# Attention: the split of new queries and the SiLU of the gates issued half a slot later, behind the emptying of the transposed weights

## The chip, the cores and the metric

The kernel runs on one core of one Trainium2 chip. The metric is the device time of one execution in microseconds (us). A core has five engines with a queue each, and an engine takes its instructions in the order in which they were issued: TensorE (PE in the rows, its weight loads PEld), VectorE (DVE), ScalarE (ACT), GpSimd (POOL) and SyncE (SP), which issues the weights' transfers.

## The reference

A trunk of two layers over 256 tokens of width 2048: a gated linear recurrence (16 heads of 128) and a sparse attention with 16 query heads in 4 groups. The change lies in the attention, whose heads compute, for each of three branches (compressed keys, selected blocks, window):

```python
logit_c = jnp.einsum('bgqhd,bgkd->bgqhk', qb, K_cmp) + bias_shared(dist_c)
p_c = masked_softmax(logit_c, (dist_c >= 0)[:, None, :])
o_c = jnp.einsum('bgqhk,bgkd->bgqhd', p_c, V_cmp)
...
gates = jax.nn.sigmoid(gate_logits.reshape(B, S, NSA_HEADS, N_BRANCH))
o = jnp.einsum('bshc,bshcd->bshd', gates, out).reshape(B, S, NSA_WIDTH) * jax.nn.silu(z)
return o.astype(h.dtype) @ w_out
```

Queries `q` and gate inputs `z` come from columns of one input projection of the layer.

## The kernel before

All large products are done with each float32 operand split into a rounded part and a rest ("hi" and "lo", or names ending in `h` and `l`), and three products hi·hi, hi·lo, lo·hi (`mm3`, L154 to L156; in the transposed projections L179 and L181).

The program is one long list `plan` of weight pieces of 128x1024 elements. `flush` (L261) goes through it; a piece is a **slot**. In a slot it calls the `done` function of a finished projection, then `advance()`, then `prefetch` (which issues the hi cast of a piece three ahead on ScalarE, L138, the lo subtraction of a piece two ahead on VectorE, L148, and loads still further ahead), then the piece's matmuls on TensorE, then `advance()` again. Side work is written as Python generators, put in a list by `run`; `advance()` takes one step, up to the next `yield`, of each generator in the list, oldest first. One `yield` is thus half a slot, and the order of issue on each engine follows from where the `yield`s stand.

In the attention part the remaining projections (queries of groups 1 to 3, gates `z` of groups 0 to 3) run as pieces, and the heads run beside them as side work: `attend(g)` (L931) for a group of 4 heads. It keeps a table `turns` of half slots, a head taking 4 slots:

- `logits` of head h in the second half of slot 4h: 9 matmuls into three PSUM banks;
- `biased` (DVE) and `exps` (ACT) in slot 4h+1, `weigh` in slot 4h+2;
- `transposes` and `evacuate` in the second half of slot 4h+3. The seven transposed blocks stand in two banks: `t1` with four 128x128 blocks, `t2` with two, and with the 47x128 block of the compressed branch. `evacuate` (L996) empties them, ACT writing `ph` (hi) and `pc`, DVE `pl` (lo) and the other rows of `pc`;
- after each pair of heads (a = 0 or 1) `values` in the next two slots: half 0 needs the `ph` and `pl` of `t1` and the `pc` of the first token half (L1029), half 1 the rest.

`logits`, `transposes` and `values` share a ring of four PSUM banks (`psa`). So a matmul that opens a bank waits until the tile that had the bank four allocations earlier has been emptied. After head 1 the issue order is `logits` of head 2, then `values`: the third logits bank is that of `t1`, and the bank of `values` is that of `t2`. After head 3 `values` comes first, then the `logits` of the next group.

Two more generators run there. When half a query projection is finished, `q_done1` (L910) copies it out of PSUM, scales it and starts `q_split` (L920): ACT casts `qh` (L854), and two half slots later DVE subtracts `ql` (L862). When a gate projection is finished, `z_done1` (L1061) does the same with `z` and starts `gated` (L1070): ACT computes the SiLU of two 128x512 tiles (L1073) with a load of the SiLU table before it, and, for the first three groups, a one-element Exp (L1076) which brings the Exp table back; then the products with the heads' outputs (DVE, L1082) and their split into `yh` (ACT, L1085) and `yl` (DVE, L1087), which the output projection reads.

Of the kernel before, what the change touches and what calls it, by code (L numbers as in the profile page):

```python
# [8 lines left out]
F32 = mybir.dt.float32  # L9
# [25 lines left out]
NCMP = (S - CMP_BLOCK) // CMP_STRIDE + 1  # L35
# [10 lines left out]
def kernel(ctx: ExitStack, tc: tile.TileContext, x, norm_gains, final_gain, rel_bias,  # L46
                             hgrn_lb, hgrn_w_in, hgrn_head_gain, hgrn_w_out, nsa_w_in, nsa_pe_k, nsa_pe_v,
                             phi_k_w1, phi_k_b1, phi_k_w2, phi_v_w1, phi_v_b1, phi_v_w2, nsa_w_out, out):
    nc = tc.nc
# [801 lines left out]
    def split_of(src, hi, lo, col=None, apart=2):  # L851
        for s_, h in zip(src, hi):
            if col is None:
                nc.scalar.copy(h, s_)  # L854
            else:
                nc.scalar.activation(h, s_, AF.Copy, scale=col[0])
                col = col[1:] + col[:1]
        for _ in range(apart):
            yield
        for s_, h, l in zip(src, hi, lo):  # L860
            if col is None:
                nc.vector.tensor_sub(l, s_, h.bitcast(F32))  # L862
            else:
                nc.vector.scalar_tensor_tensor(l, s_, col[0], h.bitcast(F32), op0=ALU.mult, op1=ALU.subtract)
                col = col[1:] + col[:1]
# [44 lines left out]
    def q_done1(g):  # L910
        def done(a, ps):
            q = zs_take(ps)
            nc.vector.tensor_mul(q, q, rbq2)
            run(q_split(g, a, q))
            if g == 0 and a == 1:
                for n in range(G):
                    run(attend(n), HEAD * G * n + 13)
        return done

    def q_split(g, a, q):  # L920
        NS["q", g, a] = [NS["p2"].tile([P, 2, S], F32R, tag="q" + part, name="q" + part, bufs=3) for part in "hl"]
        yield from split_of([q], *([t] for t in NS["q", g, a]))

# [7 lines left out]
    def attend(g):  # L931
# [64 lines left out]
        def evacuate(h):  # L996
            t1, t2 = L.pop(("t", h))
            a, hh = h // 2, h % 2
            ph, pl = pT[a]
            srcs = ((t1.rearrange("p (a t) -> p a t", a=4), slice(0, 4)),  # L1000
                    (t2[:, 0:256].rearrange("p (a t) -> p a t", a=2), slice(4, 6)))
            pc = NS["pc"][:, hh]
            for t, ks in srcs:
                nc.scalar.copy(ph[:, ks, hh, :], t)  # L1004
            for tt in range(2):
                nc.scalar.copy(pc[64:64 + NCMP, tt], t2[32 * tt:32 * tt + NCMP, 256:384])  # L1006
            for t, ks in srcs:
                nc.vector.tensor_sub(pl[:, ks, hh, :], t, ph[:, ks, hh, :].bitcast(F32))  # L1008
            nc.vector.tensor_copy(pc[0:NCMP], pc[64:64 + NCMP].bitcast(F32))
            for tt in range(2):  # L1010
                nc.vector.tensor_sub(pc[32:32 + NCMP, tt], t2[32 * tt:32 * tt + NCMP, 256:384],  # L1011
                                     pc[64:64 + NCMP, tt].bitcast(F32))

        def values(a, half):
            if half == 0:
# [25 lines left out]
        for h in range(4):  # L1041
            at(HEAD * h, 1, logits, h)
            at(HEAD * h + 1, 0, biased, h)
            at(HEAD * h + 1, 1, exps, h)
            at(HEAD * h + 2, 0, weigh, h)
            at(HEAD * h + 3, 1, transposes, h)
            at(HEAD * h + 3, 1, evacuate, h)
        for a in range(2):
            n = HEAD * (2 * a + 2)
# [11 lines left out]
    def z_done1(g):  # L1061
        def done(a, ps):
            z = zs_take(ps)
            nc.vector.tensor_mul(z, z, rb2)
            NS["z", a] = z
            if a == 1:
                run(gated(g, [NS["z", 0], z]))
        return done

    def gated(g, zs):  # L1070
        ks = [slice(4 * g + 2 * a, 4 * g + 2 * a + 2) for a in range(2)]
        for a in range(2):
            nc.scalar.activation(zs[a], zs[a], AF.Silu)  # L1073
        if g + 1 < G:

            nc.scalar.activation(NS["one"], NS["one"], AF.Exp, scale=0.0)  # L1076
        yield
        yield
        for a in range(2):
            while ("out", g, a) not in NS:  # L1080
                yield
            nc.vector.tensor_mul(zs[a], zs[a], NS["o", g][:, a])  # L1082
            yield
            yield
            nc.scalar.copy(yh[:, ks[a]], zs[a])  # L1085
            yield
            nc.vector.tensor_sub(yl[:, ks[a]], zs[a], yh[:, ks[a]].bitcast(F32))  # L1087
# [147 lines left out]
```

## Time and profile before

| | us |
|---|---|
| median of 3 runs | 986.13 |
| lowest, highest | 985.73, 987.29 |
| the profiled execution's own time | 986.4 |
| its span, first to last instruction | 984.6 |
| TensorE busy in the span | 968.7 |
| VectorE, ScalarE, GpSimd busy | 658.3, 569.5, 59.9 |
| attention heads (690 to 897 us): TensorE busy of 207 us | 200.54 |

The profiled execution took 1.8 us more than its span, and lies 0.27 us above the median of the runs. Matmuls are pipelined: a matmul's row begins before the one ahead of it has ended, so a stretch in which TensorE is always "busy" may still hide some of a wait. The rows of the weight loads (PEld) show a wait more plainly: normally one starts every 0.12 us.

### The profile page before, as it was taken

The numbers are of one execution on the slowest core, as the hardware profiler recorded it, in microseconds if no ns is written. First come the engines' busy times: TensorE is split into PE (matmuls) and PEld (weight loads), VectorE is DVE, ScalarE is ACT, GpSimd is POOL, SyncE is SP. The second block draws the span as 40 slices with busy tenths as digits, with TensorE's granted clock in tenths as the row PEclk, the third lists the DMA queues.
The fourth block names the chain that finished last, engine by engine and source line by source line (L and its number), as shares of the span: only waits on it lengthen the run. The fifth ranks groups of instructions, "written<-read, shape, count | busy, mean of one in ns | idle before, by whom it ended". The sixth has DMA issues, their size and how long they took to land.

```text
span 984.6 us, 17622 instructions
## 1 busy us (share of the span) xinstructions
PE 968.7 (98%) x6735; PEld 838.5 (85%) x6735; DVE 658.3 (67%) x1275; ACT 569.5 (58%) x1056; POOL 59.9 (6%) x154
## 2 busy tenths in 40 slices
PE   9999999999999999999999999999999999999996
PEld 8888888888888888888888888998888888888886
DVE  6796478646864786465566666567777778686654
ACT  6754565456545654554455555467677776875542
POOL 3101000100010001000020000000000000000000
PEclk9999999999999999999999999999999999999999
DMA  9655565556555655566777776565555545546662
GB/s 317 201 172 151 172 192 165 157 171 193 156 166 172 186 158 163 176 222 231 234 218 207 223 229 184 157 198 170 150 152 141 158 130 160 160 130 232 204 215 96
DMA packets 141524, 178.98 MB, mean 182 GB/s; under 512 B 6016, under 2 KB 102880, under 8 KB 141312
## 3 DMA queue, kind: packets, MB, share of 16 engines
q1 hardware_dynamic: 139424, 171.86, 56.8%
q0 software_dynamic: 1680, 5.46, 2.0%
q8 instruction: 53, 0.87, 0.4%
q10 hardware_dynamic: 336, 0.54, 0.1%
q14 instruction: 31, 0.25, 0.1%
HBM read 173.62 MB, written 4.22 MB: 181 GB/s over the span
## 4 chain that ended last, share of the span: by engine, by line
PE 80%; ACT 10%; DVE 6%; issue 2%; DMA 1%; SPq 0%; POOLq 0%; ACTq 0%; POOL 0%; DVEq 0%
PE mainps L156 40%; PE mainps L179 21%; PE mainps L181 11%; PE auxps L156 3%; ACT L L970 2%; ACT hi L138 2%; PE auxps L516 2%; DVE lo L148 1%; DVE L L963 1%; ACT ph L1004 1%; ACT L L979 1%; ACT pc L1006 1%; DMA xt<-in_x_dram 1%; DVE pc L1011 1%; ACT L1073 1%
## 5 line engine op out<-in xcount | busy, mean ns | idle before, releaser
L179 PE MATMUL mainps<-xx,hi 128*128 128x512 f32 x1280 | 454.9, 398 | 0.2 <-DVE Kg L313 0.2
L138 ACT CAST hi<-raw 128x1024 fp32r<-128x1024 f32 (+3 forms) x317 | 328.0, 1039 | 206.6 <-PE mainps L156 142.8
L148 DVE TENSOR_TENSOR lo<-raw,hi 128x1024 fp32r<-128x1024 f32 (+3 forms) x317 | 379.2, 1206 | 92.1 <-ACT hi L138 91.3
L181 PE MATMUL mainps<-xx,lo 128*128 128x256 f32 x1280 | 357.6, 279 | 0.1
L179 PEld LDWEIGHTS mainps<-xx,hi 128*128 128x128 f32 x1280 | 240.2, 188 | 54.6 <-DVE Kg L313 0.6
L181 PEld LDWEIGHTS mainps<-xx,lo 128*128 128x128 f32 x1280 | 241.4, 189 | 0.6 <-DVE lo L148 0.4
L156 PE MATMUL mainps<-hi,xx 128*128 128x512 f32 (+1 forms) x704 | 209.4, 375 | 0.0
L156 PEld LDWEIGHTS mainps<-hi,xx 128*128 128x128 f32 x704 | 128.4, 188 | 23.2
L156 PE MATMUL mainps<-lo,xx 128*128 128x512 f32 (+1 forms) x352 | 131.0, 372 | 0.0
L156 PE MATMUL mainps<-hi,yh 128*128 128x512 f32 (+1 forms) x288 | 106.0, 368 | 0.0
L156 PE MATMUL mainps<-hi,yl 128*128 128x512 f32 (+1 forms) x288 | 105.4, 366 | 0.0
L156 PE MATMUL mainps<-lo,yh 128*128 128x512 f32 (+1 forms) x288 | 105.3, 366 | 0.0
L156 PEld LDWEIGHTS mainps<-lo,xx 128*128 128x128 f32 x352 | 66.1, 188 | 10.4
L156 PEld LDWEIGHTS mainps<-hi,yl 128*128 128x128 f32 x288 | 54.3, 189 | 8.8
L156 PEld LDWEIGHTS mainps<-lo,yh 128*128 128x128 f32 x288 | 54.4, 189 | 8.5
L156 PEld LDWEIGHTS mainps<-hi,yh 128*128 128x128 f32 x288 | 54.4, 189 | 8.4
L970 ACT ACTIVATE L<-L,mx 128x128 f32<-128x128 f32 (+1 forms) x96 | 37.6, 393 | 31.0 <-DVE mx L965 31.0
L313 DVE TENSOR_TENSOR zs<-mainps,zs 128x256 f32<-128x256 f32 x48 | 19.0, 421 | 33.7 <-ACT zs L311 33.7
L567 POOL COPY ST<-S 32x128 f32<-32x128 f32 x32 | 21.6, 675 | 229.8 <-DVE S L524 228.8
L524 DVE COPY_PREDICATED S<-masks,auxps 128x128 f32<-128x128 uint32 x48 | 14.6, 303 | 28.8 <-PE auxps L557 15.9
L1008 DVE TENSOR_TENSOR pl<-auxps,ph 128x512 fp32r<-128x512 f32 (+1 forms) x32 | 17.7, 557 | 22.0 <-ACT ph L1004 20.4
L311 ACT COPY zs<-mainps 128x256 f32<-128x256 f32 x48 | 16.5, 373 | 13.5 <-PE mainps L181 13.2
(257 smaller groups left out, 905.2 us busy)
## 6 DMA issues: line engine op xcount, KB each, us to landing
raw<-in_hgrn_w_in_dram SPq DMA_DIRECT2D x127, 512.0 KB, 4.0
raw<-in_nsa_w_in_dram SPq DMA_DIRECT2D x104, 512.0 KB, 3.8
raw<-in_hgrn_w_out_dram SPq DMA_DIRECT2D x32, 512.0 KB, 4.7
raw<-in_nsa_w_out_dram SPq DMA_DIRECT2D x32, 512.0 KB, 4.0
raw<-in_nsa_w_in_dram SPq DMA_DIRECT2D x10, 420.0 KB, 3.9
xt<-in_x_dram SPq DMA_DIRECT2D x8, 256.0 KB, 7.9
raw<-in_x_dram SPq DMA_DIRECT2D x4, 512.0 KB, 4.2
x_dram<-x POOLq DMA_DIRECT2D x4, 512.0 KB, 6.0
```

Of the source, the lines that this page charges most:

```text
L138: nc.scalar.copy(hi[:, :m], raw[:, :m])
L148: nc.vector.tensor_sub(lo[:, :m], raw[:, :m], hi[:, :m].bitcast(F32))
L156: nc.tensor.matmul(dst, a, b, start=first and n == 0, stop=last and n == 2, skip_group_check=True)
L179: nc.tensor.matmul(ps, hv[:, fs], xx[:, k].rearrange("p a t -> p (a t)"), start=k == 0, stop=False, skip_group_check=True)
L181: nc.tensor.matmul(ps[:, S:], lv[:, fs], xh[:, k], start=False, stop=k == KT - 1, skip_group_check=True)
L311: nc.scalar.copy(o, p[:, S:])
L313: nc.vector.tensor_add(o, p[:, :S], o)
L516: nc.tensor.matmul(dst[32 * b:32 * b + 32, j] if cols == 32 else dst[32 * b:32 * b + 32, :, j], k[:, cs], qs, start=True, stop=True, tile_ ...
L524: nc.vector.copy_predicated(S32, masks[:, i, None, :].to_broadcast([P, 4, 32]), bank[:, n])
L567: nc.gpsimd.tensor_copy(ST[rs, :, 0:3:2, rs], S32[rs].rearrange("p (h t) c -> p h t c", h=2))
L970: nc.scalar.activation(dst, dst, AF.Exp, bias=mx[:, i:i + 1], accum_out=sm[:, i:i + 1])
L1008: nc.vector.tensor_sub(pl[:, ks, hh, :], t, ph[:, ks, hh, :].bitcast(F32))
```

## The change

Three edits, all in the order of issue. No instruction is added or taken away, and no DMA changes.

```diff
     def q_split(g, a, q):
+        yield
         NS["q", g, a] = [...]
         yield from split_of([q], *([t] for t in NS["q", g, a]))
...
-            for t, ks in srcs:
+            for n, (t, ks) in enumerate(srcs):
                 nc.scalar.copy(ph[:, ks, hh, :], t)
-            for tt in range(2):
-                nc.scalar.copy(pc[64:64 + NCMP, tt], t2[32 * tt:32 * tt + NCMP, 256:384])
-            for t, ks in srcs:
+                for tt in range(2 - 2 * n):
+                    nc.scalar.copy(pc[64:64 + NCMP, tt], t2[32 * tt:32 * tt + NCMP, 256:384])
+            for n, (t, ks) in enumerate(srcs):
                 nc.vector.tensor_sub(pl[:, ks, hh, :], t, ph[:, ks, hh, :].bitcast(F32))
-            nc.vector.tensor_copy(pc[0:NCMP], pc[64:64 + NCMP].bitcast(F32))
-            for tt in range(2):
-                nc.vector.tensor_sub(pc[32:32 + NCMP, tt], ...)
+                if n == 0:
+                    nc.vector.tensor_copy(pc[0:NCMP], pc[64:64 + NCMP].bitcast(F32))
+                for tt in range(2 - 2 * n):
+                    nc.vector.tensor_sub(pc[32:32 + NCMP, tt], ...)
...
     def gated(g, zs):
         ks = [...]
+        yield
         for a in range(2):
             nc.scalar.activation(zs[a], zs[a], AF.Silu)
```

So the `qh` cast and the SiLU block are issued in the second half of a slot instead of the first, after `evacuate` of that half slot; everything that follows them in their generators (`ql`; the products with the heads' outputs, `yh`, `yl`) moves by the same half slot. Inside `evacuate`, on both engines, the `pc` parts now stand between the part of `t1` and that of `t2`.

The lines above L921 keep their numbers; below, the changed kernel's are 2 to 5 higher (L1004 becomes L1007, L1006 L1009, L1008 L1011, L1009 L1013, L1011 L1015, L1073 L1078, L1076 L1081, L1082 L1087).

**ScalarE, from the end of a gate projection to the first half of the next head's softmax** (after head 1 of groups 1 to 3; `zs` is the projection's tile, `auxps` a bank of the ring, `one` the one-element Exp). Before:

```order
L311 COPY zs<-mainps 128x256 x2
L1073 ACT_TABLE_LOAD
L1073 ACTIVATE zs<-zs 128x512 x2
L1076 ACT_TABLE_LOAD
L1076 ACTIVATE one<-one 128x1
L138 CAST hi<-raw 128x1024
L1004 CAST ph<-auxps 128x4x128
L1004 CAST ph<-auxps 128x2x128
L1006 CAST pc<-auxps 15x128 x2
L138 CAST hi<-raw 128x1024
```

Now:

```order
L311 COPY zs<-mainps 128x256 x2
L138 CAST hi<-raw 128x1024
L1007 CAST ph<-auxps 128x4x128
L1009 CAST pc<-auxps 15x128 x2
L1007 CAST ph<-auxps 128x2x128
L1078 ACT_TABLE_LOAD
L1078 ACTIVATE zs<-zs 128x512 x2
L1081 ACT_TABLE_LOAD
L1081 ACTIVATE one<-one 128x1
L138 CAST hi<-raw 128x1024 x2
```

Four instructions and the table loads have moved from ahead of the emptying to behind it, and now stand ahead of two weight casts and of the next exponentials.

**VectorE, at the same place.** Before:

```order
L148 TENSOR_TENSOR lo<-raw,hi 128x1024
L1008 TENSOR_TENSOR pl<-auxps,ph 128x4x128
L1008 TENSOR_TENSOR pl<-auxps,ph 128x2x128
L1009 CAST pc<-pc 15x256
L1011 TENSOR_TENSOR pc<-auxps,pc 15x128 x2
L1082 TENSOR_TENSOR zs<-zs,ot 128x512
L148 TENSOR_TENSOR lo<-raw,hi 128x1024
```

Now:

```order
L148 TENSOR_TENSOR lo<-raw,hi 128x1024
L1011 TENSOR_TENSOR pl<-auxps,ph 128x4x128
L1013 CAST pc<-pc 15x256
L1015 TENSOR_TENSOR pc<-auxps,pc 15x128 x2
L1011 TENSOR_TENSOR pl<-auxps,ph 128x2x128
L148 TENSOR_TENSOR lo<-raw,hi 128x1024
L1087 TENSOR_TENSOR zs<-zs,ot 128x512
```

The two-block part of `pl` is now last, and the product with the heads' output stands behind the next weight's lo part.

**ScalarE, from the end of half a query projection** (after head 3 of groups 0 to 2). Before:

```order
L311 COPY zs<-mainps 128x256 x2
L854 CAST qh<-zs 128x512
L138 CAST hi<-raw 128x1024
L1004 CAST ph<-auxps 128x4x128
L1004 CAST ph<-auxps 128x2x128
L1006 CAST pc<-auxps 15x128 x2
```

Now:

```order
L311 COPY zs<-mainps 128x256 x2
L138 CAST hi<-raw 128x1024
L1007 CAST ph<-auxps 128x4x128
L1009 CAST pc<-auxps 15x128 x2
L1007 CAST ph<-auxps 128x2x128
L854 CAST qh<-zs 128x512
```

The `qh` cast has moved behind the emptying; the weight's hi cast stays ahead of it. On TensorE, GpSimd and SyncE all instructions keep their order.

## Rows read from the trace of the kernel before

**Rows 1.** The profile page: its first line, and section 1 (busy time of each engine, its share of the span, its instructions).

```profile
span 984.6 us, 17622 instructions
...
PE 968.7 (98%) x6735; PEld 838.5 (85%) x6735; DVE 658.3 (67%) x1275; ACT 569.5 (58%) x1056; POOL 59.9 (6%) x154
```

**Rows 2.** Busy time of each engine by stage of the span (the view of windows): the attention heads, and the tail after the last projection. Columns: stretch in us from the span's start, its length, then busy us and instructions of PE, PEld, DVE, ACT, POOL, then granted clock, DMA share, GB/s.

```profile
690.00:897.00 207.00, 200.54 (x1230) 177.34 (x1229) 157.98 (x434) 149.46 (x359) 6.33 (x20) 1.00 0.52 152
...
975.00:984.60 9.60, 2.23 (x19) 2.02 (x17) 3.34 (x9) 1.05 (x2) 0.55 (x1) 0.85 0.57 218
```

**Rows 3.** The waits of TensorE's weight loads (PEld) over the whole span, the four that lie in the attention heads: engine, line and tile, what they waited for, us in total, times, longest us.

```profile
PEld auxps L156 <- DVE pl L1008: 3.4, 6, 0.7
PEld auxps L156 <- ACT hi L138: 3.2, 3, 1.1
PEld auxps L1029 <- ACT hi L138: 2.1, 4, 0.6
...
PEld auxps L156 <- ACT ph L1004: 0.9, 2, 0.5
```

**Rows 4.** The same view for TensorE's matmuls (PE), the three longest in the attention heads.

```profile
PE auxps L156 <- DVE pc L1011: 2.7, 3, 0.9
PE auxps L156 <- DVE pl L1008: 2.0, 6, 0.5
PE auxps L1029 <- ACT hi L138: 1.4, 4, 0.4
```

**Rows 5.** Timeline of TensorE's matmuls at the first of the places called one, in the second head group: the first and the last of the seven transposes of head 1. Columns of this and the next groups: start us, us, engine, line, operation, out<-in, shapes, xcount, and in brackets the idle time of the engine before it and what ended it.

```profile
735.81 0.60 PE L990 MATMUL auxps<-ident,L 128*128 128x128 f32 x4
...
736.46 0.27 PE L993 MATMUL auxps<-ident,L 128*47 128x128 f32 x1
```

**Rows 6.** Timeline of TensorE's weight loads at the same place: the last two that run undisturbed, the two that waited, and the first of the next head's transposes.

```profile
739.77 0.19 PEld L156 LDWEIGHTS auxps<-Kl,qh 128*128 128x128 f32 x1
739.90 0.19 PEld L156 LDWEIGHTS auxps<-Kh,ql 128*128 128x128 f32 x1
740.66 0.19 PEld L156 LDWEIGHTS auxps<-Kh,qh 128*128 128x128 f32 x1 [0.57 <-DVE pl L1008]
...
742.16 0.19 PEld L156 LDWEIGHTS auxps<-ph,Vsh 128*128 128x128 f32 x1 [1.08 <-ACT hi L138]
...
752.87 0.48 PEld L990 LDWEIGHTS auxps<-ident,L 128*128 128x128 f32 x4
```

**Rows 7.** Timeline of ScalarE (ACT) at the same place.

```profile
733.85 0.65 ACT L311 COPY zs<-mainps 128x256 f32<-128x256 f32 x2
734.51 1.28 ACT L1073 ACT_TABLE_LOAD   x1
735.81 1.15 ACT L1073 ACTIVATE zs<-zs 128x512 f32<-128x512 f32 x2
...
738.37 1.03 ACT L138 CAST hi<-raw 128x1024 fp32r<-128x1024 f32 x1
739.31 0.85 ACT L1004 CAST ph<-auxps 128x512 fp32r<-128x512 f32 x2
740.17 0.53 ACT L1006 CAST pc<-auxps 15x128 fp32r<-15x128 f32 x2
...
745.64 0.40 ACT L970 ACTIVATE L<-L,mx 128x128 f32<-128x128 f32 x1 [1.27 <-DVE mx L965]
...
748.61 0.91 ACT L979 ACTIVATE L<-L,sm 128x256 f32<-128x256 f32 x2 [0.52 <-DVE sm L976]
```

**Rows 8.** Timeline of VectorE (DVE) at the same place.

```profile
735.65 1.22 DVE L148 TENSOR_TENSOR lo<-raw,hi 128x1024 fp32r<-128x1024 f32 x1
739.92 1.24 DVE L1008 TENSOR_TENSOR pl<-auxps,ph 128x512 fp32r<-128x512 f32 x2 [3.05 <-ACT ph L1004]
741.17 0.28 DVE L1009 CAST pc<-pc 15x256 fp32r<-15x256 f32 x1
741.47 0.58 DVE L1011 TENSOR_TENSOR pc<-auxps,pc 15x128 fp32r<-15x128 f32 x2
742.08 0.69 DVE L1082 TENSOR_TENSOR zs<-zs,ot 128x512 f32<-128x512 f32 x1
```

**Rows 9.** Timeline of the weight loads at the first of the places called two that has three waits, after head 3 of the same group.

```profile
770.07 0.19 PEld L156 LDWEIGHTS auxps<-ph,Vsh 128*128 128x128 f32 x1 [0.48 <-ACT ph L1004]
770.80 0.19 PEld L156 LDWEIGHTS auxps<-pl,Vsh 128*128 128x128 f32 x1 [0.54 <-DVE pl L1008]
...
772.00 0.19 PEld L1029 LDWEIGHTS auxps<-pc,Vc 79*128 79x128 f32 x1 [0.55 <-ACT hi L138]
```

**Rows 10.** Timeline of ScalarE at that place.

```profile
766.05 0.65 ACT L311 COPY zs<-mainps 128x256 f32<-128x256 f32 x2
767.97 0.62 ACT L854 CAST qh<-zs 128x512 fp32r<-128x512 f32 x1 [1.27 <-DVE zs L913]
...
769.45 0.84 ACT L1004 CAST ph<-auxps 128x512 fp32r<-128x512 f32 x2
```

**Rows 11.** Timeline of VectorE at that place.

```profile
767.85 1.22 DVE L148 TENSOR_TENSOR lo<-raw,hi 128x1024 fp32r<-128x1024 f32 x1
770.05 1.24 DVE L1008 TENSOR_TENSOR pl<-auxps,ph 128x512 fp32r<-128x512 f32 x2 [0.98 <-ACT ph L1004]
...
771.60 0.59 DVE L1011 TENSOR_TENSOR pc<-auxps,pc 15x128 fp32r<-15x128 f32 x2
```

More of the change, by code (lines that the diff above doesn't have):

```diff
@@ L1002, in evacuate @@
             pc = NS["pc"][:, hh]
-            for t, ks in srcs:
+            for n, (t, ks) in enumerate(srcs):
                 nc.scalar.copy(ph[:, ks, hh, :], t)
-            for tt in range(2):
-                nc.scalar.copy(pc[64:64 + NCMP, tt], t2[32 * tt:32 * tt + NCMP, 256:384])
-            for t, ks in srcs:
+                for tt in range(2 - 2 * n):
+                    nc.scalar.copy(pc[64:64 + NCMP, tt], t2[32 * tt:32 * tt + NCMP, 256:384])
+            for n, (t, ks) in enumerate(srcs):
                 nc.vector.tensor_sub(pl[:, ks, hh, :], t, ph[:, ks, hh, :].bitcast(F32))
-            nc.vector.tensor_copy(pc[0:NCMP], pc[64:64 + NCMP].bitcast(F32))
-            for tt in range(2):
-                nc.vector.tensor_sub(pc[32:32 + NCMP, tt], t2[32 * tt:32 * tt + NCMP, 256:384],
-                                     pc[64:64 + NCMP, tt].bitcast(F32))
+                if n == 0:
+                    nc.vector.tensor_copy(pc[0:NCMP], pc[64:64 + NCMP].bitcast(F32))
+                for tt in range(2 - 2 * n):
+                    nc.vector.tensor_sub(pc[32:32 + NCMP, tt], t2[32 * tt:32 * tt + NCMP, 256:384],
+                                         pc[64:64 + NCMP, tt].bitcast(F32))
         def values(a, half):
```

## The prediction

> **What bounds the kernel now.** I read the page first, then the busy time by stage, then who waited for whom, then the timelines at the waits. The page shows TensorE busy 968.7 of 984.6 us [rows 1]: it is the bound, and a change that neither adds nor removes work can only give back the time in which TensorE stands still. By stage, 7.4 us of that are the tail (9.60 less 2.23), which the change does not reach, and 6.5 us (207.00 less 200.54) lie in the attention heads [rows 2], where all moved instructions are. The granted clock is 1.00 there, its upper level (2.4 GHz), so no time is lost to the clock.
>
> The view of waits then names the reasons: in that stage TensorE waits for the emptying of the transposed weights, and hardly for anything else. The matmuls' rows add to 2.7 + 2.0 + 1.4 = 6.1 us [rows 4]. The weight loads' rows add to 3.4 + 3.2 + 2.1 + 0.9 = 9.6 us in 15 waits [rows 3]. I take the second: at the first wait the loads before it start 0.13 us apart (739.77, 739.90), the next at 740.66 [rows 6], so about 0.64 us were really lost, where the load's row says 0.57. A load lasts 0.19 us and normally overlaps the next one by 0.07, so each wait costs 0.07 us more than its row: 9.6 + 15 x 0.07 = **10.6 us**, all that can be won here. The Trainium skill ("Perfetto Trace Analysis", Identifying the Most-Contended Engine) has the rule for this: matmul busy time is a poor measure since matmuls are pipelined, the weight loads are the better row. By the matmuls' rows the same argument would give 986.1 - 6.1, or 980.0 us; this trace sides with the rule, by the 0.64 us against 0.57 just read.
>
> **Places one: three times, after head 1 of groups 1 to 3.** ScalarE ends the copies of the gate projection at 734.50. Then the SiLU block (table load, two SiLUs, table load, Exp) runs to 738.37, 3.9 us, then a weight cast of 1.03, and only then, at 739.31, the emptying [rows 7]. But the transposes had ended at 736.41 (first four) and 736.73 (all) [rows 5]. VectorE stood idle 3.05 us before its part [rows 8]. TensorE lost 0.57 us at the third logits bank, which was still `t1`'s, and 1.08 us at the bank of `values`, still `t2`'s [rows 6].
>
> The new order, from the same durations. ScalarE: copies to 734.50, weight cast to 735.55, then it waits for the transposes; `ph`, `pc`, `ph` from 736.45 take 0.85 + 0.53, to 737.85 (was 740.70). VectorE: its lo part ends at 736.87 [rows 8]; the first `pl` starts when the first `ph` is written. As the two casts take 0.85 us for 512 and 256 columns, I put the first at 0.6, to 737.05. From there 1.24 + 0.28 + 0.58, with seams 2.2 us, to 739.2; the `t1` part is done by 737.9. TensorE wants the third logits bank at 739.90 + 0.12 = 740.02 and, three matmuls later, the bank of `values` at 740.4. Both are free by then, with 2.1 and 1.2 us to spare. So a place one gives all of 0.57 + 1.08 + 2 x 0.07 = 1.8 us, three times 5.4.
>
> What then stands in front of other work? The SiLU block ends at 737.85 + 3.9 = 741.75, two weight casts (1.03 each) at 743.8, and the next head's exponentials can start there. They started at 745.64 before [rows 7]; as TensorE is now 1.8 us further on, that is the same place against TensorE. The later scaling had ended at 748.61 + 0.91 = 749.52, and the transposes that need it were loaded at 752.87 [rows 6, 7]: 3.3 us of room, less 0.6 for the `yh` cast that now also goes ahead of the scaling (taken as the 0.62 of `qh`, of the same shape [rows 10]). `gated`'s product on VectorE comes up at 739.2 + 1.2 (a lo part) = 740.4, when its SiLU (737.85 + 1.28 + 0.6) has just ended at 739.8, so it does not hold up the queue. The two delayed weight casts make pieces three slots ahead; they end about 1 us later than before and have over two slots of room. I cost these at nothing.
>
> The Trainium skill ("ScalarE: Activation LUTs", What ACT_TABLE_LOAD costs) speaks against this part: a switch of table costs about 1283 ns plus a drain of about 1380 ns. The row has 1.28 us and the SiLU starting 1.30 us after the load began, no drain [rows 7]. With the page's drains, an estimate, the block would be 2.8 us longer; behind the emptying it would use up the 2.7 us of room just counted. The sum would stay, the rival on the slow side would be likelier. I go by the row.
>
> **Places two: after head 3 of each group.** Before, at the second of the four: copies to 766.70, `qh` waits for VectorE and starts at 767.97, weight cast, `ph` at 769.45 [rows 10]; TensorE waits 0.48 for `ph`, 0.54 for `pl`, 0.55 for `pc` [rows 9]. New: weight cast to 767.75, first `ph` 768.3, `pc` 768.85, second `ph` 769.2. VectorE is free at 767.85 + 1.22 = 769.07 [rows 11]; by columns the first `pl` takes two thirds of 1.24, to 769.9 at the latest, the copy of `pc` 0.28, to 770.2 [rows 8], the first `pc` part 0.3, to 770.5. TensorE would come at 770.07 - 0.48 = 769.6 for `ph`, 0.12 later for `pl`, and after six loads, at 770.3, for `pc`. So `ph` is in time, and about 0.2 us remain where VectorE is now the later one. Of the four places, the first has the `pc` wait alone (its VectorE is earlier), two have all three, and the last has two; it has a SiLU block in front instead of `qh`. Together they hold 10.6 - 5.4 = 5.2 us. I leave 0.5 of it standing: 0.2 at each of the two, 0.1 at the others. The reordering inside the emptying is in this: `pc` no longer waits for the second `pl` (a third of 1.24, 0.4 us). Alone it would save that at `pc` waits only; a bank waits for the last part whatever the order.
>
> `qh` behind the emptying is needed late: these queries serve heads 2 and 3 of the next group, eight slots on. The other half's split, moved after head 2, is needed one head later. SyncE's, GpSimd's and TensorE's orders are unchanged and no DMA moves; DMA is busy 0.52 in this stage [rows 2].
>
> **Sum.** 10.6 - 0.5 = 10.1 us. Against the profiled execution, 986.4 - 10.1 = 976.3; the median of the runs is 0.27 lower, so **976.0 us**. A measurement of this kernel can tell about 0.2%, 2 us, from no change.
>
> **Rivals.** (a) *Partly*: at places two VectorE turns into the bound. For: its lo part, 1.22 us, ends 1 us before TensorE arrives. Against: 0.2 us left by the working above. If half of their 5.2 us and a little at places one stays, 7.5 us are won: 978.6. (b) *No change*: the weight cast that still stands ahead of the emptying is itself held, and the SiLU hid it. It ran at 738.37 without a recorded wait [rows 7]; were it held until then, the emptying would start as late as before. The code says that it needs a buffer freed by the piece ahead of the one whose matmuls precede the transposes at 735.81 [rows 5], so it is ready well before them. The time would be 986.1. (c) *Slower*: what was moved now delays the softmax, and the transposes come late. If there were no room, three SiLU blocks of 3.9 us and six `qh` of 0.62 would all be paid: 15.4 us against 10.1, at 991.4. It decides where the exponentials start over 2.7 us later than reckoned. Against: rows 6 and 7 show the room. That the change does not do what it says is excluded by the order of issue, which shows both moves.
>
> **How the numbers follow.** The forecast, 975.0 to 977.5, gets 0.77; (a) 0.13; (b) 0.05; (c) 0.05. The low end is all 10.6 us and 0.5 for the spread of the runs; to hold 8 in 10 the range reaches into (a), to 979.5. Faster by over 0.2%: 0.77 + 0.13 = 0.90; within: 0.05; slower: 0.05.
>
> **What would show it.** In the profile after, the four weight-load waits of rows 3 shrink from 9.6 to under 1 us; `ph` starts within 0.1 us of the first four transposes at places one; the idle 3.05 us of VectorE before `pl` is gone; TensorE is busy over 99% of the heads' stretch, which is 10 us shorter. I am wrong if waits of the same size appear at `logits` or `values` behind other names, if a weight load waits for a hi or lo part, or if the transposes wait for ScalarE's scaling.

## The result, and the profile after

| us | before | after |
|---|---|---|
| median | 986.11 | 976.56 |
| lowest, highest | 985.73, 987.29 | 975.33, 977.63 |
| the profiled execution's own time | 986.4 | 976.73 |
| its span | 984.6 | 974.9 |

The median of before is that of four runs, one more than the table ahead of the prediction had. The changed kernel is faster: the ratio of after to before is 0.9901, with a 95% interval of 0.9884 to 0.9918. The forecast was 976.0, its range 975.0 to 979.5.

The profile page after: the span, the busy times, and (section 4) the shares of the engines in the chain that ended last.

```profile
span 974.9 us, 17621 instructions
...
PE 964.1 (99%) x6735; PEld 837.4 (86%) x6735; DVE 655.8 (67%) x1275; ACT 569.0 (58%) x1056; POOL 60.0 (6%) x154
...
PE 96%; DMA 1%; DVE 1%; issue 1%; ACT 0%; SPq 0%; POOLq 0%; POOL 0%; DVEq 0%
```

The same line of the page of before:

```profile
PE 80%; ACT 10%; DVE 6%; issue 2%; DMA 1%; SPq 0%; POOLq 0%; ACTq 0%; POOL 0%; DVEq 0%
```

So ScalarE and VectorE have all but gone from the chain. By stage (view of windows, columns as in rows 2): the heads, the tail.

```profile
690.00:887.30 197.30, 197.30 (x1232) 177.09 (x1232) 156.01 (x434) 148.84 (x359) 6.35 (x20) 1.00 0.54 162
...
965.30:974.90 9.60, 1.80 (x16) 1.59 (x14) 2.91 (x8) 0.72 (x1) 0.55 (x1) 0.74 0.57 219
```

The heads' stretch is 197.3 us where it was 207.0 [rows 2], at the same granted clock of 1.00, and TensorE stands still in none of it. The tail is as long as before. The waits of the weight loads over the whole span, the first and the third longest entries (columns as in rows 3):

```profile
PEld auxps L516 <- issue: 6.0, 17, 0.8
...
PEld auxps L1198 <- DVE zeros L321: 1.1, 1, 1.1
```

None of the four entries of [rows 3] is left; what stands here lies outside the heads. Place one in the second head group, which answers to [rows 5 to 8]: TensorE's first transposes, then weight loads, ScalarE and VectorE, each in a fence of its own.

```profile
735.34 0.60 PE L992 MATMUL auxps<-ident,L 128*128 128x128 f32 x4
```

```profile
739.56 0.19 PEld L156 LDWEIGHTS auxps<-Kh,qh 128*128 128x128 f32 x1
...
739.92 0.19 PEld L156 LDWEIGHTS auxps<-ph,Vsh 128*128 128x128 f32 x1
...
750.67 0.48 PEld L992 LDWEIGHTS auxps<-ident,L 128*128 128x128 f32 x4
```

```profile
733.45 1.05 ACT L138 CAST hi<-raw 128x1024 fp32r<-128x1024 f32 x1
735.98 0.59 ACT L1007 CAST ph<-auxps 128x512 fp32r<-128x512 f32 x1 [1.47 <-PE auxps L992]
...
737.54 1.28 ACT L1078 ACT_TABLE_LOAD   x1
738.83 1.15 ACT L1078 ACTIVATE zs<-zs 128x512 f32<-128x512 f32 x2
...
741.39 1.98 ACT L138 CAST hi<-raw 128x1024 fp32r<-128x1024 f32 x2
...
743.28 0.40 ACT L972 ACTIVATE L<-L,mx 128x128 f32<-128x128 f32 x1
...
746.23 0.91 ACT L981 ACTIVATE L<-L,sm 128x256 f32<-128x256 f32 x2
```

```profile
734.72 1.22 DVE L148 TENSOR_TENSOR lo<-raw,hi 128x1024 fp32r<-128x1024 f32 x1
736.60 0.69 DVE L1011 TENSOR_TENSOR pl<-auxps,ph 128x512 fp32r<-128x512 f32 x1 [0.66 <-ACT ph L1007]
...
738.21 0.42 DVE L1011 TENSOR_TENSOR pl<-auxps,ph 128x256 fp32r<-128x256 f32 x1
```

`ph` starts 0.04 us after the first four transposes (735.94); before it was 2.9 us after them. `t1` is free at 737.29 and its bank is opened at 739.56; `t2` is free at 738.63 and the bank of `values` is opened at 739.92. So 2.3 and 1.3 us are to spare, and both loads follow 0.13 and 0.12 us behind the one before them.

Place two of the same group, which answers to [rows 9 to 11]: weight loads, then VectorE.

```profile
767.42 0.19 PEld L156 LDWEIGHTS auxps<-ph,Vsh 128*128 128x128 f32 x1
767.54 0.19 PEld L156 LDWEIGHTS auxps<-pl,Vsh 128*128 128x128 f32 x1
...
768.14 0.19 PEld L1033 LDWEIGHTS auxps<-pc,Vc 79*128 79x128 f32 x1
```

```profile
765.69 0.68 DVE L1011 TENSOR_TENSOR pl<-auxps,ph 128x512 fp32r<-128x512 f32 x1
...
766.72 0.60 DVE L1015 TENSOR_TENSOR pc<-auxps,pc 15x128 fp32r<-15x128 f32 x2
```

`pl` (done at 766.37) and `pc` (first part by 767.0) are ready some 1.1 us before TensorE asks for them, at 767.54 and 768.14. The forecast had VectorE 0.2 us late here.

To see where the time came from I set the start of every weight load after against the same load before. In the heads the difference jumps only at the 15 loads that waited: 0.54 at the first place two (a `pc` wait); 0.64 + 1.15, 0.63 + 1.16 and 0.74 + 1.16 at places one; 0.44 + 0.61 + 0.62, 0.41 + 0.61 + 0.62 and 0.46 + 0.61 at the other places two. The sum is **10.4 us**. The span is 9.7 us shorter: between the jumps the loads drift back by 0.23 us in all, in steps under 0.02; ahead of the heads the steps nearly cancel (one of 0.9 the other way at a load of L516 near 172 us, against small ones); and in the tail TensorE stood still 7.80 us instead of 7.37.

### The profile page after: what moved, and what is told of

It is laid out like the page before. It is cut to its first block, busy times and chain, and to the rows that moved or that the text cites. A ratio compares the mean times of both kernels' runs of the same rounds, so it can differ in the third digit from the quotient of the medians.

```text
span 974.9 us, 17621 instructions
## 1 busy us (share of the span) xinstructions
PE 964.1 (99%) x6735; PEld 837.4 (86%) x6735; DVE 655.8 (67%) x1275; ACT 569.0 (58%) x1056; POOL 60.0 (6%) x154
## 4 chain that ended last, share of the span: by engine, by line
PE 96%; DMA 1%; DVE 1%; issue 1%; ACT 0%; SPq 0%; POOLq 0%; POOL 0%; DVEq 0%
PE mainps L156 41%; PE mainps L179 30%; PE mainps L181 15%; PE auxps L156 5%; PE auxps L516 2%; PE auxps L992 1%; DMA xt<-in_x_dram 1%; PE auxps L582 0%; DVE lo L148 0%; DMA raw<-in_hgrn_w_in_dram 0%; PE auxps L609 0%; PE auxps L610 0%; PE auxps L591 0%; PE auxps L608 0%; PE auxps L633 0%
## 5 line engine op out<-in xcount | busy, mean ns | idle before, releaser
L1007 ACT CAST ph<-auxps 128x512 fp32r<-128x512 f32 (+1 forms) x32 | 15.4, 480 | 18.9 <-PE auxps L992 18.5
```

## The experiments

Three theories. **A**: each wait belongs to what ScalarE does in front of that emptying; the two moves give independent shares, and the reordering alone gives almost nothing. **B**: the lateness of places one carries on to places two, so one move brings most of it. **C**: the order inside the emptying does the work. "Steps" are jumps of the weight loads against before, read as above. The ratios are to runs of before on the same chip.

| kernel | median us | ratio to before (95%) |
|---|---|---|
| e1 SiLU moved alone | 980.43 | 0.9944 (0.9931 to 0.9956) |
| e2 split moved alone | 982.28 | 0.9960 (0.9947 to 0.9972) |
| e3 reordering alone | 979.71 | 0.9933 (0.9920 to 0.9945) |
| e4 both moves, old order | 976.51 | 0.9900 (0.9885 to 0.9915) |
| e5 after, block + 3 us | 980.09 | 0.9932 (0.9920 to 0.9945) |
| e6 after, block + 6 us | 989.13 | 1.0026 (1.0016 to 1.0036) |
| e7 before, block + 3 us | 998.83 | 1.0126 (1.0110 to 1.0141) |
| e8 before, no early Exp table | 988.21 | 1.0023 (1.0014 to 1.0032) |
| e9 reordering on ScalarE alone | 986.94 | 1.0007 (0.9998 to 1.0016) |
| e10 reordering on VectorE alone | 981.96 | 0.9959 (0.9946 to 0.9971) |
| e11 e3 with a copy on VectorE | 980.78 | 0.9949 (0.9936 to 0.9961) |
| e12 after with that copy | 976.51 | 0.9903 (0.9887 to 0.9918) |

### The two moves, one at a time (e1, e2, e4)

The kernel before with one `yield` in `gated` (e1), one in `q_split` (e2), or both (e4), and the old order in `evacuate`:

```diff
     def gated(g, zs):
         ks = [...]
+        yield          # e1, e4
...
     def q_split(g, a, q):
+        yield          # e2, e4
```

> Only the SiLU of the gates moves half a slot later. Theory A (each wait belongs to what stands in front of that emptying): the two waits at places one go (3 x 1.8 us in the trace) and those after head 3 of the last group, which has a SiLU in front (1.05 us); the waits after head 3 of groups 0 to 2, behind a qh cast, stay (0.6 + 1.6 + 1.6). 986.1 - 6.4 = 979.7 us. Theory B (backlog: places two are late only because ScalarE and VectorE have not caught up since place one): nearly all goes, 976.5 to 977.5. Theory C (the order inside the emptying does the work): 985 to 986.

> Only the split of new queries moves. Theory A: the places one keep their 1.8 us each, the last group keeps its 1.05 us; after head 3 of groups 0 to 2 the waits for ph and pl go, and most of that for pc: 0.6 + 1.1 to 1.6 + 1.1 to 1.6 = 2.8 to 3.8 us, 982.3 to 983.3 us. Theory B: under 1 us, 985 or more. Theory C: 985 to 986.

> Both moves, the old order inside the emptying. Theory A with the slack that the profile of the changed kernel shows (at the second place two the first pc part ends at 767.00 where its load comes at 768.14; one 0.43 us part later it is still in time): the same as the changed kernel, 976.6 us, within 0.3. If the order inside the emptying is needed besides the moves: 0.4 us at each of three or four places, 977.8 to 978.3.

The waits of the weight loads in the heads (columns as in rows 3), of e1 and then of e2:

```profile
PEld auxps L1029 <- ACT hi L138: 1.6, 3, 0.5
...
PEld auxps L156 <- DVE pl L1008: 1.1, 2, 0.5
...
PEld auxps L156 <- ACT ph L1004: 0.9, 2, 0.5
```

```profile
PEld auxps L156 <- ACT hi L138: 3.2, 3, 1.1
PEld auxps L156 <- DVE pl L1009: 2.3, 4, 0.7
...
PEld auxps L1030 <- ACT hi L138: 0.6, 1, 0.6
```

Against [rows 3], e1 has lost the three waits of about 1.1 at `values`, four of the six for `pl` and one of the four for `pc`: places one, and the last group's place two, which also has a SiLU block in front. The waits of the other places two are all there. e2 has kept exactly those that e1 lost. The steps are 6.55 and 3.83 us and add to all of the 10.4 (by the medians 5.7 and 3.9, against 9.6 for the whole change). That is what A says of the two moves, and it excludes B: a place two keeps its whole wait when place one ahead of it is mended. e4, both moves in the old order, equals after within its spread, with the same steps (10.4) and no such wait left: beside the moves the reordering is worth nothing that can be measured.

### The reordering alone, and half of it at a time (e3, e9, e10)

e3 is after without its two `yield`s; e9 and e10 are before with the new order on one engine:

```diff
 # e9: ScalarE
-            for t, ks in srcs:
+            for n, (t, ks) in enumerate(srcs):
                 nc.scalar.copy(ph[:, ks, hh, :], t)
-            for tt in range(2): ...               # pc, behind the second ph
+                for tt in range(2 - 2 * n): ...   # pc, ahead of the second ph
 # e10: VectorE
-            for t, ks in srcs:
+            for n, (t, ks) in enumerate(srcs):
                 nc.vector.tensor_sub(pl[...], ...)
-            nc.vector.tensor_copy(pc[0:NCMP], ...)
-            for tt in range(2): ...               # pc, behind the second pl
+                if n == 0: nc.vector.tensor_copy(pc[0:NCMP], ...)
+                for tt in range(2 - 2 * n): ...   # pc, ahead of the second pl
```

> Only the order inside the emptying changes (pc ahead of the second part of ph and pl). Theory A: nothing at places one, where a whole bank is waited for; at the four pc waits VectorE gets there one 0.43 us part sooner: 1.7 us at most, 984.4 to 986.1 us. Theory C: most of the gain, 977 to 979.

> The kernel before, with the new order inside the emptying on ScalarE alone (pc copies ahead of the second ph); VectorE keeps its old order. If VectorE's order made the gain of the reordering (pc parts and pl no longer in each other's way on a bank), nothing is won here: pl of t2 now waits about 0.1 us for the second ph instead of for pc, and 985.5 to 986.5 is expected, with the pc waits in place. If ScalarE's order made it, the time is that of the reordering on both, 979.3 to 980.3. If both are needed or each brings a part, something between, with the other half in the second kernel.

> The kernel before, with the new order inside the emptying on VectorE alone (pc parts ahead of the second pl); ScalarE keeps its old order. If VectorE's order made the gain of the reordering, 979.5 to 980.5: its first pl ends 1.30 us after the first ph starts, the pc copies 1.39 us after, so the pc parts can follow with a seam of 0.1 at most, the pc waits (0.6 at each of seven places) go, and the queues run earlier as with the reordering on both. If ScalarE's order made it, 985.5 to 986.5 here, less the pc waits that VectorE's earlier pc parts take away, at most 3.

e3 missed A's expectation by over 4 us: the reordering alone brings two thirds of the gain. Its steps are not at `pc` only (0.54, 0.57, 0.58, 0.61), but also 0.46 to 0.47 at the third logits bank of each place one and 0.41 to 0.46 at the `ph` and `pl` loads of places two. The `values` banks kept about 1.0 each. e9 and e10 put it on VectorE's order: alone it brings 4.3 us, ScalarE's alone nothing; the other 2.2 us of e3 come only with both. (981.96 of e10 lies between the two outcomes written down for it, so it bears out VectorE's order in part.) VectorE's emptying at the same place one, of e9, e10 and e3 (before: rows 8, from 739.92 to the next instruction at 742.08):

```profile
741.34 0.69 DVE L1008 TENSOR_TENSOR pl<-auxps,ph 128x512 fp32r<-128x512 f32 x1 [3.04 <-ACT ph L1004]
742.28 0.42 DVE L1008 TENSOR_TENSOR pl<-auxps,ph 128x256 fp32r<-128x256 f32 x1 [0.25 <-ACT ph L1004]
...
743.62 0.69 DVE L1082 TENSOR_TENSOR zs<-zs,ot 128x512 f32<-128x512 f32 x1
```

```profile
738.52 0.69 DVE L1008 TENSOR_TENSOR pl<-auxps,ph 128x512 fp32r<-128x512 f32 x1 [3.05 <-ACT ph L1004]
...
740.22 0.42 DVE L1008 TENSOR_TENSOR pl<-auxps,ph 128x256 fp32r<-128x256 f32 x1
740.56 0.68 DVE L1083 TENSOR_TENSOR zs<-zs,ot 128x512 f32<-128x512 f32 x1
```

```profile
738.70 0.69 DVE L1009 TENSOR_TENSOR pl<-auxps,ph 128x512 fp32r<-128x512 f32 x1 [3.05 <-ACT ph L1005]
...
740.64 0.68 DVE L1084 TENSOR_TENSOR zs<-zs,ot 128x512 f32<-128x512 f32 x1
```

From the first `pl` to the next instruction VectorE takes 2.16 us before, 2.28 in e9, 2.04 in e10 and 1.94 in e3. The instructions last as long in all; the seams differ. When the two-block `pl` is last, the next instruction starts 0.08 before its end; when a `pc` part is last, 0.03 after it. And with the new order on both, VectorE no longer waits about 0.12 after the first `pl` for ScalarE (e9 makes that wait 0.25, for the second `ph`). A second seam goes with the first: behind the lo part that follows the emptying, the first `biased` instruction (L963) starts 0.03 us after that part's end in before and e9, and 0.08 before it in e10 and e3.

A measure of what this is worth to the next head is how long ahead of the place-one transposes VectorE's lo part starts: 0.16 us before [rows 5, 8], 0.17 in e9 (737.08 against 737.25), 0.41 in e10 (734.25 against 734.66), 0.63 in e3 (734.43 against 735.06). The third logits bank gained 0.02, 0.25 and 0.47, as much as the lead (0.01, 0.25, 0.47). (In e9 the 0.12 more in the emptying falls into idle time ahead of that lo part.) One head is enough for this lead: after head 0 of the group the first `pl` starts 1.25 to 1.26 us after the first transposes began in all four, for there VectorE still waits for ScalarE's `ph`. The row of before:

```profile
723.89 1.23 DVE L1008 TENSOR_TENSOR pl<-auxps,ph 128x512 fp32r<-128x512 f32 x2 [1.01 <-ACT ph L1004]
```

The lead grows on to head 3: at place two the lo part starts 1.69 us behind the transposes in before and 0.82 in e3. At the next group's head 0 VectorE waits again, so it does not grow from group to group (0.46 to 0.47 at all three places one).

### VectorE's queue loaded again (e11, e12)

```diff
+        NS["pad"] = n1.tile([P, 96], F32, name="pad")
...
         # end of evacuate: e3's (e11), after's (e12)
+            nc.vector.tensor_copy(NS["pad"], NS["pad"])
```

> The reordering alone on both engines, plus one copy of a scratch tile of 96 columns onto itself on VectorE behind every emptying (about 0.25 us, some 0.2 of it on VectorE's queue; 16 times). Theory: VectorE's queue is full between two emptyings, the reordering makes each emptying 0.1 shorter on it and lets the next instruction start 0.1 earlier, 0.2 a head, and this backlog, not the order in which banks come free, gave the gains at the third logits bank and at the ph loads (0.4 each, six places). Then those 2.5 us come back, while the pc waits (0.6 each, four places) stay gone: 982 to 984. Rival: the gain lies in the order in which the parts come free, and 0.2 us on VectorE changes nothing: 979.5 to 980.5.

> The changed kernel with the same scratch copy on VectorE behind every emptying. With the blocks behind the emptyings VectorE's parts end over 1 us before TensorE asks for them, so 0.2 us a head cost nothing: 976.3 to 977.3. If VectorE were within 0.2 us of being late anywhere, up to 3 us more: 979.5.

The copy lasted 0.20 and pushed the next instruction by 0.12, less than meant. e11 gave 1.1 us back of e3's gain, a miss by the numbers expected: 980.78 is 1.2 us under the theory's range and only 0.3 above the rival's, and the intervals of e11's and e3's ratios overlap. So the median does not tell the two apart; the steps do. e11's lead is 0.50 and its step at the third logits bank 0.34 to 0.35, each 0.13 less than in e3; the `pl` loads of places two gained 0.22 and 0.25 where e3 gained 0.41 to 0.43; the `pc` steps are as in e3 (0.54 to 0.59). So time on VectorE's queue comes back at the places named, about as much as was added. e12 cost nothing, 976.51: behind the moves VectorE has the time.

### How much the block costs on either side (e5, e6, e7)

More table switches behind the SiLU block, one extra pair (2.97 us) in e5 and e7, two (5.94) in e6:

```diff
             nc.scalar.activation(NS["one"], NS["one"], AF.Exp, scale=0.0)
+            for _ in range(1):          # 2 in e6
+                nc.scalar.activation(NS["one"], NS["one"], AF.Silu, scale=0.0)
+                nc.scalar.activation(NS["one"], NS["one"], AF.Exp, scale=0.0)
```

> The changed kernel with two more table loads and two one-element activations behind each of the first three SiLU blocks (about 2.97 us more of ScalarE's queue each, from the rows 1.28 and 0.2). If the block behind the emptying lies in room, as the prediction costed it (2.7 us of room before the next transposes): the same as the changed kernel, or up to 0.3 us per block more: 976.6 to 977.5 us. If the moved block is already at the edge: 3 x 2.97 = 8.9 us more, 985.5.

> The same with 5.94 us more per block. With 2.7 us of room, 3.2 us per block go over it: 976.6 + 9.7 = 986.3 us, and the trace shows TensorE waiting at the transposes after head 2 or for a weight's hi or lo part. If the room is larger than reckoned (all slack of three slots): 977 to 980.

> The kernel before with the same 2.97 us added to the SiLU block, which there stands ahead of the emptying. If the emptying behind it is what TensorE waits for, each us of it is paid in full: 986.1 + 8.9 = 995.0 us. If the waits had another cause (a held weight cast, VectorE), it costs less: under 990.

e5 and e6 missed. Against after they cost 3.5 and 12.6 us, 1.2 and 4.2 for each block. From e5 to e6 all of the 2.97 us is paid (3.0 a block); 2.97 less 1.2 and 5.94 less 4.2 both say, as an estimate, that behind the emptying a block has some **1.75 us of room**, not 2.7. By the steps of the weight loads (4.4 and 13.5 us) it is 1.5; no smaller block was run. What it runs into in e5 (waits of the weight loads; then the first load of each of the two):

```profile
PEld mainps L181 <- DVE lo L148: 2.4, 4, 0.8
PEld auxps L156 <- DVE pl L1011: 2.1, 3, 0.8
```

```profile
752.31 0.19 PEld L181 LDWEIGHTS mainps<-xx,lo 128*128 128x128 f32 x1 [0.72 <-DVE lo L148]
...
769.05 0.19 PEld L156 LDWEIGHTS auxps<-pl,Vsh 128*128 128x128 f32 x1 [0.81 <-DVE pl L1011]
```

VectorE ahead of the first of them, in after and then in e5:

```profile
742.46 1.23 DVE L148 TENSOR_TENSOR lo<-raw,hi 128x1024 fp32r<-128x1024 f32 x1 [0.59 <-ACT hi L138]
...
748.04 1.22 DVE L148 TENSOR_TENSOR lo<-raw,hi 128x1024 fp32r<-128x1024 f32 x1
```

```profile
745.45 1.23 DVE L148 TENSOR_TENSOR lo<-raw,hi 128x1024 fp32r<-128x1024 f32 x1 [3.63 <-ACT hi L138]
...
751.04 1.22 DVE L148 TENSOR_TENSOR lo<-raw,hi 128x1024 fp32r<-128x1024 f32 x1
```

The longer block holds up the hi cast of the next weight on ScalarE; VectorE's queue stands 3.63 us for it instead of 0.59, and all that follows there is 3.0 us later. The next weight's lo part, behind the softmax, ended 2.3 us before its load in after (749.26 against 751.55); now TensorE waits 0.72 for it, not for the transposes. The other half is lost at the next place two: VectorE is still 2.0 us later there against TensorE, the `pl` that had 1.17 us to spare is late, and TensorE waits 0.81. In e6 the lo part's entry is 8.3 us in 7 waits, that for the hi part 2.1 in 3, and the transposes wait 1.0 us in all.

e7 shows the other side: ahead of the emptying every microsecond is paid. The step at the third logits bank is 3.03 us at each of the three places. The run is 12.8 us slower than before, not 8.9; this is the rest, at the first of the three places (weight loads; then windows, columns as in rows 2):

```profile
744.09 0.19 PEld L156 LDWEIGHTS auxps<-Kh,qh 128*128 128x128 f32 x1 [3.60 <-DVE pl L1008]
...
745.59 0.19 PEld L156 LDWEIGHTS auxps<-ph,Vsh 128*128 128x128 f32 x1 [1.08 <-ACT hi L138]
...
746.30 0.33 PEld L156 LDWEIGHTS auxps<-ph,Vwl 128*128 128x128 f32 x1
```

```profile
736.00:744.00 8.00, 4.71 (x32) 4.07 (x30) 1.93 (x3) 7.88 (x14) 0.12 (x1) 1.00 0.39 121
...
746.20:749.40 3.20, 3.20 (x13) 2.81 (x13) 3.13 (x15) 1.92 (x4) 0.00 (x0) 0.50 0.24 46
749.40:753.00 3.60, 3.60 (x26) 3.34 (x25) 3.30 (x10) 3.05 (x15) 0.00 (x0) 1.00 0.78 241
```

After standing 3.6 and 1.1 us TensorE was granted 0.50 (1.2 GHz) for 3.2 us, and a load lasts 0.33 us instead of 0.19. While this lasts the steps add to 1.6 us here, and to 2.1 and 2.3 at the two later places; the places two gave 1.2, 1.2 and 0.5 back.

### A shorter block in the old place (e8)

```diff
-        if g + 1 < G:
-            nc.scalar.activation(NS["one"], NS["one"], AF.Exp, scale=0.0)
```

> The kernel before without the one-element Exp at the end of the SiLU block: the Exp table is then loaded ahead of the next exponentials, and the block ahead of the emptying is 1.48 us shorter (1.28 + 0.2). The computation is complete. By the same theory 1.48 of the 1.8 us go at each of the three places one: 4.4 us, 981.7 us, unless the table load then delays the exponentials (room 2.7 us, so no). If the block is not what TensorE waits for: 986.

A miss, slower than before. Places one gained as reckoned, 0.6 to 0.7 and 0.8 to 0.9. But the Exp table is now loaded when the exponentials of head 2 are due, and what that delays is the emptyings behind, that of place two above all (waits of the weight loads; ScalarE; the heads' window):

```profile
PEld auxps L156 <- ACT ph L1004: 4.3, 3, 1.5
```

```profile
744.96 1.28 ACT L970 ACT_TABLE_LOAD   x1 [1.25 <-DVE mx L965]
```

```profile
690.00:900.00 210.00, 204.05 (x1233) 180.37 (x1233) 158.33 (x435) 149.63 (x356) 6.36 (x20) 0.98 0.54 152
```

The `ph` waits grew from 0.9 [rows 3] to 4.3 us, and after the longer waits the granted clock fell (0.98 over the stretch, 1.00 before). In the old arrangement ScalarE has no room at places two.

## Why the prediction was right

- **The bound and the sum.** TensorE's waits in the heads were all there was to win, and all of it was won: 10.4 us by steps, against 10.1 forecast. The 10.6 us counted 15 waits with 0.07 of overlap each, 0.2 too much (three of these loads still have 0.04 of idle time ahead of them after the change); and the 0.5 left at places two did not stay. So 0.3 more was won than forecast, while the drift of 0.23 and, in the profiled execution, a tail with 0.43 more of standing were not forecast and took some back; the medians differ by 9.6 us. That the result lies as near as 0.6 is in part luck. The weight loads' rows were the right ones: the matmuls' rows would have given 6.1 us. The prediction's 0.64 against 0.57 did not show that, as both are read from weight loads; the 10.4 does.
- **Places one: right, by mechanism and size.** 1.79, 1.79 and 1.90 us each against 1.8; e1 shows that the SiLU block's place alone does it. The spare times reckoned, 2.1 and 1.2 us, came out at 2.3 and 1.3. VectorE's idle 3.05 [rows 8] is 0.66, the rest of it a wait for a `ph` that is itself on time.
- **Places two: right mechanism, one term wrong.** e2 shows that the `qh` casts made these waits, and e1 that the SiLU block made the last group's. The 0.5 us that VectorE was to keep is 0. The step that failed took VectorE's free time, 769.07, from the trace of before. There the lo part ended 2.0 us after the last transpose (767.09); in after it ends at 765.78, 0.9 after it (764.88). So the queue that the step held fixed runs 1.1 us earlier against TensorE, which is more than the 0.2 missing. 0.7 of it comes with the split (e2 and e4 have it, e1 0.1 only): the other half's `qh` stood in the same way in front of the emptying after head 2, one head earlier (`ph` there starts 1.90 us after the first transposes began, in e2 0.63). The other 0.4 is the new order (after against e4); e4, without it, has no wait left either. No run moved the two `qh` one by one.
- **What was costed at nothing** cost nothing, but the room was misjudged. The exponentials start at 743.28, as reckoned (743.8, with all 0.47 us earlier in after). The next scaling ends at 747.14 and its transposes are loaded at 750.67, 3.5 us, near the 3.3 of the prediction; yet the block has some 1.75 us, for what gives way first is a weight's lo part on VectorE, behind the delayed cast and the softmax, which I had given "over two slots", and then the `pl` of place two (e5). The Trainium skill ("ScalarE: Activation LUTs", What ACT_TABLE_LOAD costs) adds a drain to each switch of table, 2.8 us a block by its figures, an estimate. No run here shows one: the row after has 1.28 and the SiLU starts 1.29 behind the load's start, as in [rows 7]. Had the drains been there, e5 gives the price, an estimate: about 3 us back.
- **The reordering: wrong.** "Alone it would save that at `pc` waits only" fell with e3: it brings 6.5 us (6.1 by steps). I looked at what frees a bank and not at what the order does to VectorE's own queue, 0.1 to 0.2 us in each emptying and 0.12 at the seam behind it (e9, e10, e11). Beside the moves these gains overlap with theirs, so the sum was not touched (e4).
- **The rivals.** (a) did not occur: no wait for VectorE is left. (b) is out: the cast that stays ahead ran at 733.45, well before the transposes. (c) is out for this block, but e6 shows that it exists: with 6 us more in each block the change is slower than before.

## What to carry to other kernels

When the emptying of a bank holds up TensorE, look at what stands in front of it on the emptying engine's queue; work that is needed later can go behind it, and each microsecond in front is paid in full (e7) while behind it some 1.5 to 1.75 were free (an estimate from e5 and e6). Seams of 0.1 us are worth more than they look on a queue that has no time to catch up: here the lead grew to 0.47 us in one head and 0.87 in three; measure how far ahead of TensorE that queue runs, not only the waits. Gains found by separate edits need not add: by steps the two moves did (6.6 and 3.8 give 10.4), the reordering and the moves did not (6.1 and 10.4 give 10.4).

## What was not expected of the hardware

- After waits of 3.6 and 1.1 us close together TensorE ran at a granted 0.50 for 3.2 us and then at 1.00 again (e7); the waits of 0.6 and 1.1 in before left it at 1.00 [rows 2].
- Where VectorE's last instruction of the emptying is a `pc` part of 15 partitions the next one starts 0.03 us after it, behind a two-block `pl` 0.08 before its end; both orders have the same instructions and durations. No run settles why.
- Single loads at L516 wait 0.6 to 1.0 us with no cause in the profile in some profiled executions and not in others (after, e1, e9 against e2, e3, e10): a step of 0.9 us in one profile is no effect of a change by itself.
